# Head 0's scan: its four projection blocks spread over the head's whole window

## The chip, the cores and the metric

The kernel runs on one core of one Trainium2 chip. The metric is the device time of one execution in microseconds (us), median of several runs. A core has five engines with a queue each: TensorE (PE, matmuls and transposes into PSUM), VectorE (DVE), ScalarE (ACT), GpSimd (POOL) and SyncE (SP, which here only issues transfers). Each works through its own queue in order, and they wait for one another by semaphores. A matmul has its own row for loading the weights (PEld).

## The reference

Two layers of a trunk run over 640 tokens of width 1024: 128 context tokens and 512 latent tokens (five chunks of 128; chunk 0 is the context). Layer 0 mixes positions with a gated MLP. Layer 1 is a bidirectional gated DeltaNet with 8 heads, d_k = 128, d_v = 256:

```python
qkv = jax.nn.silu(short_conv(qkv, conv_w)).astype(jnp.float32)   # width 5, centred
q = l2norm(q.reshape(B, N, H_B, D_K)) * (D_K ** -0.5)
k = l2norm(k.reshape(B, N, H_B, D_K))
...
sol = lax.linalg.triangular_solve(lhs, rhs, left_side=True, lower=True)
...
def step(S, xs):
    qk_i, qd_i, kd_i, u_i, w_i, gl_i = xs
    v_new = u_i - jnp.einsum('bhcd,bhde->bhce', w_i, S)
    o = jnp.einsum('bhcd,bhde->bhce', qd_i, S) + jnp.einsum('bhij,bhje->bhie', qk_i, v_new)
    S = S * gl_i[..., None, None] + jnp.einsum('bhcd,bhce->bhde', kd_i, v_new)
    return S, o
```

Both directions are scanned and added; the sum is normalised, gated with SiLU(z), projected out, and added to the residual before the last layer norm.

## The kernel before

Layer 1 works head by head. Per head there are four projection blocks of 128 output columns (q = 0 for k, 1 for q, 2 and 3 for the two halves of v) and two more for the gate z (q = 4, 5). The parts are generators, each cut into pieces at its `yield`s:

- `project_head` and `project_z` (17 turns): a block is 2 halves of the tokens x 8 slices of the input width. One piece is `mm3`, three matmuls of 128x320 (L235, L236, L237) with weights split into a high and a low part. After each half ACT copies the sum out of PSUM (L831, L832, L834) into `xp`. In the second half the next block's weights are split, high part by ACT (L230) and low part by DVE or POOL (L231); the raw weights come through SP (L166) into three buffers.
- `conv`: ACT's first tap (L845), four taps on DVE (L848), a tanh on ACT (L851) and the SiLU's end on DVE (L853), which writes `cacc`.
- `post_k`, `post_q`, `post_v`: transposes of `cacc` on PE (L240, in `flip`), norms (sums of squares L876 on ACT, L246 on DVE, the power L248 on POOL, L905 on DVE), and a store of k and v per token (L907, L941).
- `chunk`, for three groups of chunks of a head: Gram matrices (L964), decays (L967, L969 on DVE) and the inverse of the triangular matrix in six doubling steps. One step is a product on PE (L1018), masks on DVE (L1023, tile Y), products on PE (L1029, L1030), a copy by ACT (L1033, tile TU). Corrections and the matrices G (L1003, L1042, L1048 to L1076) stand before and after the steps.
- `scan`, in five steps of two units (one per direction): PE reads the state (L1113), DVE makes r (L1116), PE applies G (L1126, L1127), DVE updates the state and the output (L1135, L1141, L1121). SP loads the state (L1093) and v (L1098); `chunk` loads the decays ex (L958) and kn (L961).

`stages()` lays these parts on a time axis whose unit is one head's window: window w holds the scan of head w, the chunks of head w + 1, the projections of head w + 2, and the end of head w - 1. The projection blocks of a window lie in equal slots, from `START[w + 2]` sixths of the window to its end; `conv` begins when its block ends, one sixth long, and the `post` part one sixth later. `turns()` sorts all pieces by their time, and the generators are called in that order. For PE and SP this order of calls is the queue's order (`manual_schedule`); the queues of DVE, ACT and POOL are put in order by the framework from the same program. The weights are loaded in the order in which blocks stand on the axis.

The window of head 0 (w = 0) has four blocks, those of head 2, since ZW places z blocks at w = -1 and from w = 1 on; windows 1 to 5 have six.

Of the kernel before, what the change touches and what calls it, by code (L numbers as in the profile page):

```python
# [77 lines left out]


ZW, ZPOS = (-1, 1, 2, 3, 4, 5, 6, 6), 0  # L80
START = 2, 0.3, 1
PIECES = {"scan": 24, "chunk": 40, "norm_o": 4, "gate_z": 4, "conv": 8, "post_k": 13,
          "post_q": 7, "post_v": 5, "gates": 7, "gates_e": 26, "residual": 17}

# [1 line left out]
def stages():  # L86
# [5 lines left out]
    for w in range(-2, H + 1):  # L92
# [7 lines left out]
        else:  # L100
            slots[ZPOS:ZPOS] = zs
        start = START[w + 2] if w + 2 < len(START) else 0
        wide = (n - start) / len(slots) if slots else 0
# [1318 lines left out]
```

## Time and profile before

| | us |
|---|---|
| median of 3 runs | 1349.68 |
| the runs | 1349.72, 1349.68, 1346.47 |
| the profiled execution | 1356.16 |
| its span (first to last instruction) | 1354.3 |
| PE busy | 1285.2 (95%) |
| DVE, ACT, POOL busy | 852.5, 601.4, 509.1 |

The profile's page gives the busy time of each engine; its other views give who waited for whom, the busy time and the granted PE clock of any stretch, and the instructions in order of time. Times in these views are us from the start of the span. PE's queue reaches head 0's window shortly before 670 us, and the next window's scan begins at 752 us (the first L1126 there starts at 752.29). Matmuls are pipelined: the distance between the starts of two of them says more than the length given for one.

### The profile page before, as it was taken

The numbers are of one execution on the slowest core, as the hardware profiler recorded it, in microseconds if no ns is written. First come the engines' busy times: TensorE is split into PE (matmuls) and PEld (weight loads), VectorE is DVE, ScalarE is ACT, GpSimd is POOL, SyncE is SP. The second block draws the span as 40 slices with busy tenths as digits, with TensorE's granted clock in tenths as the row PEclk, the third lists the DMA queues.
The fourth block names the chain that finished last, engine by engine and source line by source line (L and its number), as shares of the span: only waits on it lengthen the run. The fifth ranks groups of instructions, "written<-read, shape, count | busy, mean of one in ns | idle before, by whom it ended". The sixth has DMA issues, their size and how long they took to land. (4 is left out here: it accounts for less than half of the span.)

```text
span 1354.3 us, 22840 instructions
## 1 busy us (share of the span) xinstructions
PE 1285.2 (95%) x8773; PEld 1139.6 (84%) x8773; DVE 852.5 (63%) x1599; ACT 601.4 (44%) x1432; POOL 509.1 (38%) x503
## 2 busy tenths in 40 slices
PE   7999999999999998998989999999999999989996
PEld 4688899999997887787878999989899998877785
DVE  3664644444446566798667677686777767656357
ACT  2333522222224334675636555564555556453230
POOL 0221322222223433355243636356474745520014
PEclk9999999999999999999989999999999999999998
DMA  8512233333335323143122322324243243545732
GB/s 337 168 63 86 93 134 125 125 125 125 125 125 203 124 82 141 63 125 95 50 84 73 122 87 64 106 86 153 82 133 113 82 129 90 157 124 166 260 117 78
DMA packets 90254, 163.18 MB, mean 120 GB/s; under 512 B 9088, under 2 KB 55456, under 8 KB 90016
## 3 DMA queue, kind: packets, MB, share of 16 engines
q1 hardware_dynamic: 88704, 156.99, 35.3%
q10 hardware_dynamic: 1440, 4.72, 1.0%
q8 instruction: 69, 1.13, 0.3%
q14 instruction: 41, 0.34, 0.1%
HBM read 135.97 MB, written 25.71 MB: 119 GB/s over the span
## 5 line engine op out<-in xcount | busy, mean ns | idle before, releaser
L231 POOL TENSOR_TENSOR wlo<-wraw,whi 128x256 fp32r<-128x256 f32 (+1 forms) x188 | 198.4, 1078 | 249.7 <-ACT whi L230 249.6
L235 PE MATMUL pp<-hThi,whi 128*128 128x320 f32 (+1 forms) x784 | 278.8, 356 | 0.2 <-ACT hThi L230 0.2
L237 PE MATMUL pp<-hTlo,whi 128*128 128x320 f32 (+1 forms) x784 | 243.4, 311 | 0.4 <-POOL hTlo L231 0.4
L236 PE MATMUL pp<-hThi,wlo 128*128 128x320 f32 (+1 forms) x784 | 242.9, 310 | 0.0
L230 ACT CAST whi<-wraw 128x256 fp32r<-128x256 f32 (+1 forms) x262 | 142.9, 594 | 86.3 <-PE pacc L236 60.2
L235 PE MATMUL pacc<-hThi,whi 128*128 128x320 f32 x512 | 159.6, 312 | 0.0
L237 PE MATMUL pacc<-hTlo,whi 128*128 128x320 f32 x512 | 158.3, 309 | 0.0
L236 PE MATMUL pacc<-hThi,wlo 128*128 128x320 f32 x512 | 158.2, 309 | 0.0
L848 DVE SCALAR_TENSOR_TENSOR cacc<-xp,convw,cacc 128x642 f32<-128x642 f32 x128 | 137.1, 1071 | 31.2 <-ACT cacc L845 29.7
L235 PEld LDWEIGHTS pp<-hThi,whi 128*128 128x128 f32 (+1 forms) x784 | 148.0, 189 | 3.7 <-ACT hThi L230 0.3
L236 PEld LDWEIGHTS pp<-hThi,wlo 128*128 128x128 f32 (+1 forms) x784 | 147.7, 188 | 3.9
L237 PEld LDWEIGHTS pp<-hTlo,whi 128*128 128x128 f32 (+1 forms) x784 | 146.6, 187 | 1.6 <-POOL hTlo L231 0.7
L231 DVE TENSOR_TENSOR wlo<-wraw,whi 128x1024 fp32r<-128x1024 f32 (+1 forms) x74 | 89.6, 1222 | 65.2 <-ACT whi L230 65.0
L248 POOL TENSOR_TENSOR rs<-ve,mhalf 128x1 f32<-128x1 f32 (+2 forms) x39 | 40.1, 1028 | 176.1 <-DVE ve L246 172.8
L235 PEld LDWEIGHTS pacc<-hThi,whi 128*128 128x128 f32 x512 | 96.1, 188 | 3.1 <-issue 2.2
L236 PEld LDWEIGHTS pacc<-hThi,wlo 128*128 128x128 f32 x512 | 96.1, 188 | 0.0
L237 PEld LDWEIGHTS pacc<-hTlo,whi 128*128 128x128 f32 x512 | 96.1, 188 | 0.0
L256 POOL TENSOR_SCALAR gsq<-gsq 128x320 f32<-128x320 f32 (+1 forms) x52 | 27.7, 533 | 136.5 <-ACT gsq L255 135.6
L257 DVE TENSOR_TENSOR gsq<-pacc,gsq 128x320 f32<-128x320 f32 (+1 forms) x52 | 29.1, 565 | 73.7 <-POOL gsq L256 73.6
L255 ACT ACTIVATE gsq<-pacc 128x320 f32<-128x320 f32 (+1 forms) x52 | 25.7, 499 | 107.8 <-PE pacc L237 103.8
L1033 ACT CAST TU<-pt 128x512 f16<-128x512 f32 (+1 forms) x120 | 57.2, 526 | 30.0 <-PE pt L1030 27.6
L235 PE MATMUL pacc<-whi,hThi 128*128 128x512 f32 x160 | 64.1, 412 | 5.5 <-ACT whi L230 4.3
(334 smaller groups left out, 2987.8 us busy)
## 6 DMA issues: line engine op xcount, KB each, us to landing
wraw<-in_w_b SPq DMA_DIRECT2D x48, 512.0 KB
wraw<-in_w_ada SPq DMA_DIRECT2D x37, 512.0 KB
wraw<-in_w_uz SPq DMA_DIRECT2D x32, 512.0 KB
v<-kvd SPq DMA_DIRECT2D x72, 128.0 KB
wraw<-in_a_wo SPq DMA_DIRECT2D x16, 512.0 KB
wraw<-in_b_wo SPq DMA_DIRECT2D x16, 512.0 KB
kvd<-nat SPq DMA_DIRECT2D x24, 320.0 KB
cacc<-yd SPq DMA_DIRECT2D x24, 320.0 KB
```

Of the source, the lines that this page charges most:

```text
L230: self.nc.scalar.copy(hi, src)
L231: (e_lo or self.nc.vector).tensor_tensor(lo, src, f32(hi), op=ALU.subtract)
L235: mm(out, l_hi, r_hi, start=start, stop=False)
L236: mm(out, l_lo, r_hi, start=False, stop=False)
L237: mm(out, l_hi, r_lo, start=False, stop=stop)
L248: nc.gpsimd.tensor_tensor(r, ve, self.mhalf[:, 0:n], op=ALU.pow)
L255: nc.scalar.activation(sq, u, AF.Square)
L256: nc.gpsimd.tensor_scalar(sq, sq, GB, 1.0, op0=ALU.mult, op1=ALU.add)
L257: nc.vector.tensor_tensor(sq, u, sq, op=ALU.mult)
L848: nc.vector.scalar_tensor_tensor(acc, xp[:, i : i + PADN], w[:, i : i + 1], acc, op0=ALU.mult, op1=ALU.add)
L1033: nc.scalar.copy(part, p.rearrange("p s k t (j b) -> p s (k t j) b", b=b))
```

## The change

One number: the third entry of `START` goes from 1 to 0.

```diff
 ZW, ZPOS = (-1, 1, 2, 3, 4, 5, 6, 6), 0
-START = 2, 0.3, 1
+START = 2, 0.3, 0
 PIECES = {"scan": 24, "chunk": 40, "norm_o": 4, "gate_z": 4, "conv": 8, "post_k": 13,
```

For window 0 the four blocks had slots of 1.25 sixths (1.0 to 2.25, to 3.5, to 4.75, to 6.0) and now have 1.5 sixths (0 to 1.5, to 3.0, to 4.5, to 6.0). The convolutions of the first three follow at 1.5, 3.0 and 4.5 in place of 2.25, 3.5 and 4.75; the last block ends as before. No instruction is added or removed by intent; outside window 0 the axis is the same.

PE, from the second pair of Gram matrices (L964) of head 1's chunks in the window, over the scan's first units. Before:

```order
L964 MATMUL pt_6507<-kq_5849 128x2x128 x2
L1126 MATMUL ps_6510<-v_6470,G_1036_6329 128x256
L1127 MATMUL ps_6510<-v_6470,G_1036_6329 128x256
L1126 MATMUL ps_6513<-v_6470,G_1036_6329 128x256
L1127 MATMUL ps_6513<-v_6470,G_1036_6329 128x256
L1003 LDWEIGHTS A_1072_6500
L1003 MATMUL pt_6545<-id_759_4865,A_1072_6500 128x128
```

Now (pp is the PSUM sum of a projection block, pp_6455 and pp_6556 are the two halves of head 2's k block):

```order
L964 MATMUL pt_6531<-kq_5849 128x2x128 x2
L1126 MATMUL ps_6534<-v_6476,G_1036_6329 128x256
L1127 MATMUL ps_6534<-v_6476,G_1036_6329 128x256
L1126 MATMUL ps_6537<-v_6476,G_1036_6329 128x256
L1127 MATMUL ps_6537<-v_6476,G_1036_6329 128x256
L235 MATMUL pp_6455<-hThi_64,whi_6399 128x320
L236 MATMUL pp_6455<-hThi_64,wlo_6400 128x320
L237 MATMUL pp_6455<-hTlo_65,whi_6399 128x320
L235 MATMUL pp_6556<-hThi_64,whi_6399 128x320
L236 MATMUL pp_6556<-hThi_64,wlo_6400 128x320
L237 MATMUL pp_6556<-hTlo_65,whi_6399 128x320
```

Seven pieces of the first half now stand ahead of this L964 (between it and the L1064 before it), where there was none; five more follow up to the transposes of head 1's last v block (L240 on cacc), where there was one. From that L240 to the end of the window 52 pieces are left in place of 63.

DVE, at the convolution (L848, L853) of that same block and the decays of head 1's chunks (L967, L969, L974). Before:

```order
L967 TENSOR_TENSOR ge_1078_6517<-pt_6507,ex_6455 128x256
L848 SCALAR_TENSOR_TENSOR cacc_6453<-xp_766_4887,convw_4867,cacc_6453 128x642
L969 TENSOR_TENSOR pe_1079_6519<-pt_6507,ex_6455 128x256
L848 SCALAR_TENSOR_TENSOR cacc_6453<-xp_766_4887,convw_4867,cacc_6453 128x642
L974 SCALAR_TENSOR_TENSOR A_1080_6521<-ge_1078_6517,beta_4873,masks_4857 128x128
```

Now:

```order
L848 SCALAR_TENSOR_TENSOR cacc_6459<-xp_766_4887,convw_4867,cacc_6459 128x642 x3
L967 TENSOR_TENSOR ge_1080_6546<-pt_6531,ex_6461 128x256
L848 SCALAR_TENSOR_TENSOR cacc_6459<-xp_766_4887,convw_4867,cacc_6459 128x642
L969 TENSOR_TENSOR pe_1081_6548<-pt_6531,ex_6461 128x256
L974 SCALAR_TENSOR_TENSOR A_1082_6550<-ge_1080_6546,beta_4873,masks_4857 128x128 x4
L853 SCALAR_TENSOR_TENSOR cacc_6459<-xp_766_4887,cacc_6459 128x642
L1141 TENSOR_TENSOR o_6478<-o_6478,ps_6537 128x256
```

Three of the four taps stand ahead of the decays, and the scan's L1141, which stood ahead of L853, stands behind it. Later in the window one L246 (of head 2's k) stands between the second and the third of three L1023, where it stood behind all three, and one L848 stands right ahead of an L1023 of a late inversion step.

SP, where the scan's and the chunks' first loads are issued. Before:

```order
L961 DMA kn_1058_6457<-kvd_4835 128x128
L1093 DMA S_6466<-in_state 128x256
L1093 DMA S_6468<-in_state 128x256
L1098 DMA v_6470<-kvd_4834 128x256
L166 DMA wraw_6314<-in_w_b 128x1024
L941 DMA kvd_4835<-nat_6343 640x1x128
```

Now:

```order
L166 DMA wraw_6314<-in_w_b 128x1024
L166 DMA wraw_6453<-in_w_b 128x1024
L958 DMA ex_6461<-ed_4833 128x5x128
L961 DMA kn_1060_6463<-kvd_4835 128x128
L1093 DMA S_6472<-in_state 128x256
L1093 DMA S_6474<-in_state 128x256
L1098 DMA v_6476<-kvd_4834 128x256
L941 DMA kvd_4835<-nat_6343 640x1x128
```

Two weight blocks now go ahead of these loads, where one went behind them; the second (wraw_6453) takes the buffer of a block whose low part POOL splits, and waits for that. The load of ex, which stood further ahead, stands among them.

## The prediction

> **What bounds the kernel now.** I read the page first, for the engine that is nearly always busy, then the waits of that engine, then its time around the largest one.
>
> ```profile
> span 1354.3 us, 22840 instructions
> PE 1285.2 (95%) x8773; PEld 1139.6 (84%) x8773; DVE 852.5 (63%) x1599; ACT 601.4 (44%) x1432; POOL 509.1 (38%) x503
> ```
>
> TensorE (PE) is busy for 95% of the span, the next engine for 63%. The kernel gets shorter where PE waits or runs slowly. The change moves work in head 0's scan, so I asked for busy time from 669 us (its first matmuls) on, and for PE's waits there. Columns of the first view: window, its length, busy us (count) of PE, PEld, DVE, ACT and POOL, granted PE clock, DMA share, GB/s; of the second: who waited for whom, total us, times, longest.
>
> ```profile
> 669.00:740.00 71.00, 61.20 (x481) 55.29 (x480) 51.27 (x106) 38.03 (x105) 27.80 (x27) 0.93 0.26 81
> 690.00:740.00 50.00, 47.24 (x420) 43.75 (x418) 35.71 (x79) 26.57 (x73) 17.34 (x17) 1.00 0.29 88
> 740.00:820.00 80.00, 78.64 (x626) 73.47 (x626) 56.11 (x121) 45.40 (x132) 37.24 (x41) 1.00 0.28 90
> ```
>
> ```profile
> PE px L240 <- DVE cacc L853: 6.7, 1, 6.7
> PE pt L1029 <- DVE Y L1023: 1.8, 1, 1.8
> PE pt L1048 <- DVE U L1042: 0.9, 1, 0.9
> PE pt L1074 <- DVE T L1067: 0.4, 1, 0.4
> ```
>
> From 669 to 740 us PE stands idle for 71.0 - 61.2 = 9.8 us, and one wait makes 6.7 of them: the transposes (L240) of head 1's last block wait for the end of its convolution (L853) on VectorE (DVE). The next 80 us, where projection matmuls lie between the scan's pieces from the first on, lose 1.4 us. The 669 stretch also has a granted clock of 0.93:
>
> ```profile
> 677.00:678.00 1.00, 0.00 (x0) 0.00 (x0) 1.00 (x2) 0.02 (x1) 1.00 (x2) 0.97 0.88 209
> 678.00:682.00 4.00, 0.00 (x0) 0.00 (x0) 4.00 (x5) 0.74 (x1) 3.69 (x5) 0.50 0.52 177
> 682.00:688.00 6.00, 5.66 (x18) 4.76 (x19) 2.96 (x6) 2.23 (x6) 2.86 (x2) 0.50 0.00 0
> 688.00:689.00 1.00, 1.00 (x6) 0.83 (x6) 0.39 (x2) 0.47 (x1) 0.00 (x0) 0.91 0.00 0
> ```
>
> The clock halves 0.97 us into the 677 window and is full again 0.18 us into the 688 window. PE works from 682.34 to 688.18 at half clock: 5.84 us for 2.9 us of work. So the one stall costs 6.7 + 2.9 = 9.6 us, 0.7% of the span.
>
> **The change part by part.** *Fill moved into the stall.* One projection piece (L235 to L237, three matmuls) takes from one L235 to the next; the timeline of PE (start, us, line):
>
> ```profile
> 667.28 0.30 PE L235 MATMUL pp<-hThi,whi 128*128 128x320 f32 x1
> 667.72 0.31 PE L235 MATMUL pp<-hThi,whi 128*128 128x320 f32 x1
> ...
> 669.49 0.65 PE L964 MATMUL pt<-kq 128*128 128x256 f32 x2
> ...
> 675.00 0.39 PE L235 MATMUL pp<-hThi,whi 128*128 128x320 f32 x1
> ...
> 682.34 1.11 PE L240 MATMUL px<-ident,cacc 128*128 128x128 f32 x4 [6.66 <-DVE cacc L853]
> ```
>
> That is 0.44 us. In the order of before, one piece stands between L1064 and the waiting L240; in the changed order 12 do. So 11 x 0.44 = 4.8 us of PE work move ahead of the wait. Their weights are no new wait: in the old order their first piece already ran at 675.00, and the split that makes them ended on DVE at 660.7:
>
> ```profile
> 659.26 1.43 DVE L231 TENSOR_TENSOR wlo<-wraw,whi 128x256 fp32r<-128x256 f32 x4
> ```
>
> *When PE now gets to L240.* From 669.49 to 675.00 PE had 5.5 us, 0.4 of it the wait for T, so 5.1 us of work. With 12 pieces it is 5.1 + 5.3 = 10.4 us: L240's turn comes at 679.9, where it came at about 675.7.
>
> *When its input is ready.* DVE and ScalarE (ACT) before the wait:
>
> ```profile
> 672.52 0.84 ACT L845 ACTIVATE cacc<-xp,convw 128x642 f32<-128x642 f32 x1
> 673.39 0.42 DVE L967 TENSOR_TENSOR ge<-pt,ex 128x256 f32<-128x256 f32 x1 [1.76 <-PE pt L964]
> ...
> 680.18 0.41 DVE L1141 TENSOR_TENSOR o<-o,ps 128x256 f32<-128x256 f32 x1
> 680.51 1.78 DVE L853 SCALAR_TENSOR_TENSOR cacc<-xp,cacc 128x642 f32<-128x642 f32 x1
> ```
>
> DVE works without a gap from 673.39 to 682.29: 8.9 us. In the new order L967 waits for a later matmul (its L964 comes after 7 pieces instead of none, 7 x 0.44 = 3.1 us less the 0.4 of waiting that they fill), but three L848 stand ahead of it, which need only L845, and L1141 goes behind L853. The same 8.9 us less L1141's 0.4 start with L848 at 673.4 and end at 681.9. The wait that is left is 681.9 - 679.9 = 2.0 us, 4.7 us less than now. Bounds: L853 took 1.78 us here and 0.83 us at 736.91 (below), so 1.0 us if it runs unhindered; 2.9 us if the later L967 lets DVE idle for as long as one L848 (0.88, at 718.47 below). I take 2.0: **-4.7 us**. The 0.4 us wait for T goes too, since pieces now stand before L1074: **-0.4 us**.
>
> ```profile
> 680.34 1.26 POOL L989 TENSOR_TENSOR A<-A,ident 128x512 f16<-128x512 f32 x1 [0.23 <-DVE A L974]
> 736.91 0.83 DVE L853 SCALAR_TENSOR_TENSOR cacc<-xp,cacc 128x642 f32<-128x642 f32 x1 [0.27 <-ACT xp L851]
> ```
>
> The long L853 starts while GpSimd (POOL) runs L989; the short one runs with POOL idle. [...] The sum keeps 1.78.
>
> *The clock.* With 2.0 us of waiting in place of 6.7 I take the half-clock stretch as gone: **-2.9 us**. It is the least sure term, and a rival below.
>
> *What the fill leaves behind.* The 4.8 us of pieces are missing between the steps after L240: 52 in place of 63 up to the end of the window, about one in six. There PE waited for 50 - 47.24 = 2.8 us. A step of the chunk inversion goes L1018, L1023 on DVE, L1029, L1033 on ACT, next L1018; where PE's filled time is longer than DVE's or ACT's, a missing piece costs nothing; where it is not, all 0.44 us come back as waiting. The one step that already waits shows how:
>
> ```profile
> 718.08 0.47 DVE L1121 SCALAR_TENSOR_TENSOR o<-ps,scal,o 128x256 f32<-128x256 f32 x1
> 718.47 0.88 DVE L848 SCALAR_TENSOR_TENSOR cacc<-xp,convw,cacc 128x642 f32<-128x642 f32 x1
> 719.26 0.94 DVE L1023 TENSOR_TENSOR Y<-pt,wm 128x256 f16<-128x256 f32 x3
> ```
>
> Convolution and scan updates stand ahead of the three L1023 in DVE's queue. The new order has two places like it that the old one has not: L246, which waits for four sums of squares on ACT, stands before the last of three L1023, and an L848 stands ahead of the L1023 of a late step. I price each at 1 us, and a third at the same for what I do not see: **+3.0 us**. Bounds: 0 (all slack) and 4.8 (every removed piece comes back).
>
> *SyncE's queue.* The load of a weight block (L166) now stands ahead of ex, kn, S, S and v for the scan, and waits for POOL's split that frees its buffer:
>
> ```profile
> 651.36 4.14 POOL L231 TENSOR_TENSOR wlo<-wraw,whi 128x256 fp32r<-128x256 f32 x4 [12.70 <-ACT whi L230]
> 660.78 0.69 ACT L986 ACTIVATE M<-kn,scal 128x128 f32<-128x128 f32 x2
> 663.25 0.37 ACT L1039 CAST U<-pt 128x256 f16<-128x256 f32 x1 [1.28 <-PE pt L1064]
> 725.75 0.42 SPq L166 DMA_DIRECT2D wraw<-in_w_b  x1
> 731.00:732.00 1.00, 1.00 (x15) 0.88 (x14) 1.00 (x4) 0.35 (x1) 1.00 (x2) 1.00 0.15 51
> ```
>
> The split ends at 655.5, and only then do the six loads go out. The same row of loads, in the same order, left SyncE (SPq) from 725.75 on, and its last bytes moved in the 731 window, where 51 GB/s are left: under 6 us. So all have landed by 661.5. The first to need one is ACT's L986 (kn), whose turn comes at 660.78; behind it ACT idles 1.28 us before L1039, which PE needs. A kn that lands by 661.5 is hidden by that: **0**. Were it later than 662.1, every us would reach PE.
>
> *Sum.* -4.7 - 0.4 - 2.9 + 3.0 = -5.0 us: a span of 1349.3. The profiled execution took 1356.16 us, 1.9 more than its span, and lies 6.5 above the median of 1349.68; a difference of this kind has no reason to scale with that, so I take it off the median: **1344.7 us**.
>
> **The rivals.** *All slack.* None of the removed pieces is missed: the +3.0 becomes 0, 1341.7 us. For it: in the old order one step in the whole window waits for L1023. Against: the two places in DVE's new order.
>
> *All given back.* Each removed piece comes back as waiting, +4.8 in place of +3.0: 1346.5 us. For it: the scan's own chain (L1113, L1116, L1126, L1135) is the same length as before; against: PE has 47.24 busy us of 50 there, so steps are paced by PE and not by the chain.
>
> *The clock falls all the same.* A wait before another transpose shows it (the row of 718 us holds the 1.8 us wait for L1023):
>
> ```profile
> 541.50 1.97 PE L240 MATMUL ptr<-ident,r 128*128 128x128 f32 x8 [2.68 <-DVE oh L621]
> 541.00:545.00 4.00, 3.50 (x16) 2.89 (x16) 2.74 (x10) 3.59 (x8) 2.88 (x3) 0.57 0.32 114
> 718.00:720.00 2.00, 0.27 (x7) 0.27 (x7) 2.00 (x6) 0.49 (x2) 0.65 (x1) 1.00 0.00 0
> ```
>
> After 2.7 us of waiting the mean clock over 4.0 us was 0.57: half of it for 3.4 us. After 1.8 us it stayed at 1.00. My 2.0 us lies between. If it falls so, up to half of 3.4 is lost: 1344.7 + 1.7 = 1346.4 us. [...]
>
> *DVE becomes the bound* (the slower side). The window then holds three convolutions in full, each closer to the inversion steps. If in each of the eight steps after L240 the L1023 stand behind such work as the one at 719.26, PE waits 1.8 us eight times: 14.4 in place of 3.0, 1344.7 + 11.4 = 1356.1 us. It decides from 8.0 / 8 = 1.0 us a step, where the gain of 8.0 us (4.7 + 0.4 + 2.9) is used up. Against: DVE is busy 35.71 of 50 us; with the window some 8 us shorter that would be 85%.
>
> **How the numbers follow.** Forecast (with waits after L240 of 1.5 to 4 us, so 1343.2 to 1345.7) 0.45; all slack 0.13; all given back 0.17; clock falls 0.17; DVE bound 0.08. What can be told from no change is 0.3%, 4.05 us: faster means below 1345.6. To it belong three quarters of the forecast (its upper end and the spread of the runs before, 1346.47 to 1349.72, take the rest), all of the all-slack case and a sixth of the next two: 0.34 + 0.13 + 0.05 = 0.52. Slower than 1353.7 is most of the last case, 0.07. The rest, 0.41, is the same. The range goes from 1340.5 (1.2 under the all-slack case, if L240's wait falls to its lower bound) to 1350.0 (given back and clock together, 1348.2, with the spread of the runs).
>
> **What would show it.** Right: PE's wait for L853 before L240 between 1.0 and 2.9 us; the granted clock 1.00 from 669 to 740; new waits of PE on L1023 of about 1 us, 5 to 6 us of idle time in that window's later part, and the same waits as now after it; the six loads issued in one row behind a POOL split, with no wait of ACT's L986. Wrong: a wait for L853 of 4 us or more, or the clock at 0.50 behind it; PE waits of over 8 us in all after L240; PE waiting for L1048 early on behind a late kn; a total that moves although this window does not.

## The result, and the profile after

| | before | changed kernel |
|---|---|---|
| median of 6 runs each, us | 1349.70 | 1342.11 |
| the runs, us | 1346.47 to 1352.97 | 1340.34 to 1344.92 |
| ratio, with its 95% interval | | 0.9937 [0.9923, 0.9952] |
| profiled execution and its span, us | 1356.16, 1354.3 | 1341.76, 1340.0 |

The change makes the kernel 6.5 to 10.4 us faster (the interval times 1349.7 us); the forecast was 5 us (1344.7, within 1340.5 to 1350.0). The direction was right, the size too small. One further execution of the changed kernel, in the run e9_after below, took 2101.59 us at a mean granted clock of 0.56; the ratios are those of the other executions.

The two profiled executions differ by more than the medians, 14.4 us, because the one of before lay 6.5 us above its median. To tell the change from that, I take one stretch of the program in every profile: from the start of the 158th L235 of a projection (tile pp, weights whi on the right side) to the start of the 317th. It holds head 0's whole window and begins before the first reordered piece; outside it PE has the same order in both kernels. PE alone, in the columns window, its length, busy us (count), granted clock, DMA share, GB/s; before and after:

```profile
655.86:804.26 148.40, 137.80 (x1098) 0.97 0.25 78
```

```profile
650.54:790.64 140.10, 136.17 (x1099) 1.00 0.29 89
```

The stretch is **8.3 us** shorter. That is the change; it agrees with the ratio (0.63% of 1349.7 us is 8.5 us). The other 6 us between the two profiles lie outside it. PE's waits in it, after (the four rows of before that the prediction shows, and 0.6 us for L1030, are their counterpart):

```profile
PE pt L1018 <- DVE TU L1005: 1.1, 1, 1.1
PE px L240 <- DVE cacc L853: 0.8, 1, 0.8
PE pt L1030 <- DVE Y L1023: 0.6, 1, 0.6
PE pt L1029 <- DVE Y L1023: 0.6, 2, 0.3
PE pt L1048 <- ACT U L1039: 0.5, 1, 0.5
```

The 6.7 us before L240 have become 0.8, and nothing of that size has come in their place: idle time in the stretch falls from 10.6 to 3.9 us. The 71 us that answer to the prediction's first window (all five engines) have a full clock:

```profile
664.00:735.00 71.00, 67.75 (x541) 61.58 (x541) 54.22 (x119) 44.85 (x130) 33.23 (x33) 1.00 0.25 73
```

PE was busy for 61.20 us there and is now for 67.75. Around the stall, in order of time on PE, DVE and POOL (start, us, engine, line; in brackets the idle time ahead of it):

```profile
669.45 1.02 PE L964 MATMUL pt<-kq 128*128 128x256 f32 x4
...
675.34 0.66 PE L240 MATMUL px<-ident,cacc 128*128 128x128 f32 x4 [0.76 <-DVE cacc L853]
```

```profile
667.88 3.38 DVE L848 SCALAR_TENSOR_TENSOR cacc<-xp,convw,cacc 128x642 f32<-128x642 f32 x3 [1.25 <-ACT cacc L845]
671.18 0.41 DVE L967 TENSOR_TENSOR ge<-pt,ex 128x256 f32<-128x256 f32 x1
...
674.47 0.81 DVE L853 SCALAR_TENSOR_TENSOR cacc<-xp,cacc 128x642 f32<-128x642 f32 x1
675.20 0.41 DVE L1141 TENSOR_TENSOR o<-o,ps 128x256 f32<-128x256 f32 x1
```

```profile
674.62 1.80 POOL L989 TENSOR_TENSOR A<-A,ident 128x512 f16<-128x512 f32 x1 [0.75 <-DVE A L974]
```

Times of the two profiles are 5.32 us apart at the stretch's start (655.86 and 650.54). On the clock of before, PE's turn at L240 comes at 675.34 - 0.76 + 5.32 = 679.9, where the forecast put it to the tenth. L853 ends at 675.28 + 5.32 = 680.6, 1.3 us earlier than forecast: it starts 0.15 us ahead of POOL's L989 and takes 0.81 us (1.78 before), and this time L989 is the long one, with 1.80 us (1.26 before).

### The profile page after: what moved, and what is told of

It reads as the page before. It is cut to its first block, busy times and chain, and to the rows that moved or that the text cites. A ratio compares the mean times of both kernels' runs of the same rounds, so it can differ in the third digit from the quotient of the medians.

```text
span 1340.0 us, 22836 instructions
## 1 busy us (share of the span) xinstructions
PE 1277.5 (95%) x8773; PEld 1133.2 (85%) x8773; DVE 851.0 (64%) x1599; ACT 600.6 (45%) x1432; POOL 509.9 (38%) x503
## 5 line engine op out<-in xcount | busy, mean ns | idle before, releaser
L235 PE MATMUL pp<-hThi,whi 128*128 128x320 f32 (+1 forms) x784 | 279.2, 356 | 0.2 <-ACT hThi L230 0.2
L235 PE MATMUL pacc<-hThi,whi 128*128 128x320 f32 x512 | 159.6, 312 | 0.0
L848 DVE SCALAR_TENSOR_TENSOR cacc<-xp,convw,cacc 128x642 f32<-128x642 f32 x128 | 137.1, 1071 | 32.0 <-ACT cacc L845 30.6
L235 PEld LDWEIGHTS pp<-hThi,whi 128*128 128x128 f32 (+1 forms) x784 | 147.5, 188 | 3.8 <-ACT hThi L230 0.3
L235 PEld LDWEIGHTS pacc<-hThi,whi 128*128 128x128 f32 x512 | 96.1, 188 | 3.1 <-issue 2.2
L235 PE MATMUL pacc<-whi,hThi 128*128 128x512 f32 x160 | 63.1, 406 | 5.5 <-ACT whi L230 4.1
```

The lines of the kernel that those rows point to most:

```text
L235: mm(out, l_hi, r_hi, start=start, stop=False)
L848: nc.vector.scalar_tensor_tensor(acc, xp[:, i : i + PADN], w[:, i : i + 1], acc, op0=ALU.mult, op1=ALU.add)
```

## The experiments

All runs are compared with the kernel before on the same chip. "Stretch" is the one defined above: 148.4 us before, 140.1 after. The diffs are cut (`...`), and each is against the kernel that its row names, before or changed; those of `START` are against the kernel before.

| run | what it is | ratio to before | stretch, us | wait at L240, us |
|---|---|---|---|---|
| e5_warm | before, PE kept busy in the stall | 0.9988 [0.9975, 1.0000] | 146.8 | 0 |
| e1_post_late | before, L240 later | 0.9992 [0.9977, 1.0007] | 146.3 | 0 |
| e2_half | START[2] = 0.5 | 0.9970 [0.9955, 0.9986] | 145.8 | 3.8 |
| e6_dve_order | changed, L853 late on DVE | 0.9951 [0.9934, 0.9968] | 144.7 | 3.7 |
| e4_fill_only | changed, conv and post as before | 0.9921 [0.9903, 0.9938] | 140.0 | 0.8 |
| e3_front | changed, last sixth empty | 0.9967 [0.9950, 0.9983] | 144.6 | 0 |
| e7_thin | changed, pieces earlier still | 0.9940 [0.9924, 0.9955] | 138.2 | 0 |
| e8_thinner | the same, more so | 0.9961 [0.9947, 0.9975] | 143.6 | 0 |
| s1 | START = 2, 0, 0 | 0.9949 [0.9931, 0.9967] | 140.0 | 0.8 |
| s2 | START = 1.5, 0, 0 | 0.9969 [0.9955, 0.9983] | 140.0 | 0.8 |
| e9_after | the changed kernel again | 0.9932 [0.9918, 0.9946] | 140.0 | 0.8 |
| e10_thin | e7_thin again | 0.9928 [0.9914, 0.9942] | 138.4 | 0 |

### The clock by itself

```diff
-    def flip(self, src, c0):
+    def flip(self, src, c0, warm=0):
...
+        for c in [c - warm for c in warms] + list(range(n)):
+            self.transpose(p[:, c % n, :], self.ident if c < 0 else src(c0 + c), self.ident)
...
+            p = self.flip(lambda c: s[:, tok(c)], c0, 60 * ((h, q, c0) == (1, 3, 1)))
```

> The kernel before, with 60 more transposes of the identity into the same PSUM tile just ahead of the waiting L240 (their results are overwritten), about 6.2 us of PE work that stands where PE waits now. The end of L853 on VectorE stays where it is. Theory (the clock falls because PE is idle, and costs 2.8 us by itself): the granted clock stays at 1.00 from 669 to 740 us, L240 starts at the same distance from the scan's start, and the time falls by 2.5 to 3 us. Rival (the half clock costs nothing that lasts, since PE would wait for VectorE behind it anyhow): clock 1.00, new waits of 2 to 3 us behind L240, the time the same within 0.7 us.

PE of this kernel in order of time, and its granted clock:

```profile
673.07 6.71 PE L240 MATMUL px<-ident 128*128 128x128 f32 x60
679.93 0.66 PE L240 MATMUL px<-ident,cacc 128*128 128x128 f32 x4
```

```profile
653.42:697.44 44.02, 43.48 (x347) 1.00 0.26 82
...
715.00:719.00 4.00, 3.97 (x22) 0.57 0.25 67
```

The real transposes start 679.93 - 653.42 = 26.51 us into the stretch (26.48 in the kernel before), so VectorE was no earlier. The clock stayed full, and PE reached the 197th piece after 44.02 us; the kernel before needs

```profile
655.86:702.67 46.81, 39.77 (x287) 0.89 0.25 77
```

46.81 us. The half clock behind the stall costs **2.8 us** by itself, as the theory has it: nothing behind L240 waits longer for it. The ratio shows less (1.6 us, interval 0 to 3.4), and in this profile the reason can be seen: at 715 us a wait of 1.8 us for L1023, as long as it is in the kernel before, was followed by 3.4 us at half clock, which it was not there. Of the 2.8 us, 1.2 were lost again by that in this execution.

### The place of L240

```diff
-                add(("post_k", "post_q", "post_v", "post_v")[q], (h, q), (i + POST_AT) / n,
-                    (i + POST_AT + (KLEN if q == 0 else POST_LEN)) / n)
+                add(("post_k", "post_q", "post_v", "post_v")[q], (h, q), (i + POST_AT + 0.8 * ((h, q) == (1, 3))) / n,
+                    (i + POST_AT + 0.8 * ((h, q) == (1, 3)) + (KLEN if q == 0 else POST_LEN)) / n)
```

> The kernel before, with only the post part of head 1's last block (its transposes L240) 0.8 sixths later on the axis, so that 12 projection pieces stand ahead of it as in the changed kernel; no piece is moved. Theory (PE lacks work that does not depend on VectorE there; VectorE's row from L967 to L1005 is what is late): the wait before L240 goes, but PE now runs on to the next product that needs VectorE, L1018 on TU, and waits there 4 to 6 us; the clock halves as before; gain 0 to 2 us. Rival (the place of this one L240 is the whole cause): no wait over 2 us in its neighbourhood, clock full, gain 7 to 9 us.

PE's largest waits, and its time at half clock:

```profile
PE ps L1113 <- DVE o L1141: 3.7, 1, 3.7
PE pt L1029 <- DVE Y L1023: 1.8, 1, 1.8
PE pt L1018 <- DVE TU L1005: 1.5, 1, 1.5
```

```profile
679.52:686.35 6.83, 4.99 (x14) 0.50 0.29 104
```

The gain is 1.1 us by the ratio, whose interval holds no gain too, and 2.1 in the stretch. L240 waits no more, but 3.7 + 1.5 = 5.2 us of waiting come back at the next instructions that need VectorE. The first is one I had not named: L1113, which needs the PSUM tile that L1141 has still to read. Then comes L1018, as expected. So no single instruction is to blame: VectorE's row is late, and PE has nothing else to do. The rival falls.

### VectorE's order alone

```diff
-                add("conv", (h, q), (i + CONV_AT) / n, (i + CONV_AT + CONV_LEN) / n)
+                add("conv", (h, q), (i + CONV_AT) / n, (i + CONV_AT + CONV_LEN + 0.1 * ((h, q) == (1, 3))) / n)
```

> The changed kernel with one difference, on VectorE alone: the convolution of head 1's last block ends a tenth of a sixth later on the axis, so that L853 stands behind L1141 and L980, no longer right behind L974. PE, ScalarE, GpSimd and SyncE have the same order as in the changed kernel. Theory (what is left of the stall is VectorE's row alone, and L853's place in it carries a part of the gain): L853 ends 1.8 to 2.7 us later, PE's wait before L240 goes from 0.8 to 2.5 to 3.5 us, the clock may halve for one stretch of 3.4 us; time 1.8 to 4.5 us above the changed kernel. Rival (PE would wait at L1018 for TU anyhow, so L853's place is free): waits of L240 and L1018 together as in the changed kernel, time within 0.7 us of it.

DVE, then PE's wait, then the clock in PE's rows:

```profile
676.32 0.41 DVE L1141 TENSOR_TENSOR o<-o,ps 128x256 f32<-128x256 f32 x1
676.65 1.63 DVE L980 TENSOR_TENSOR M<-pe,masks 128x512 f32<-128x512 f32 x1
678.21 1.78 DVE L853 SCALAR_TENSOR_TENSOR cacc<-xp,cacc 128x642 f32<-128x642 f32 x1
```

```profile
PE px L240 <- DVE cacc L853: 3.7, 1, 3.7
```

```profile
677.52:680.93 3.41, 0.89 (x7) 1.00 0.82 267
680.93:684.34 3.41, 3.41 (x10) 0.50 0.00 0
```

With every projection piece where the changed kernel has it, two instructions ahead of L853 on VectorE take back 4.6 of the 8.3 us: 2.9 us of waiting, and most of the rest the half clock behind it. Both the wait of 3.7 us and the 4.6 us lie a little above the theory's bounds (3.5 and 4.5). L853 ends 3.0 us later in the stretch than in the changed kernel, and 1.0 of them is its own length: POOL's L991 starts at 677.81, 0.4 us ahead of it, and L853 takes 1.78 us in place of 0.81. The rival (L853's place is free) falls. The gain is therefore not that of the pieces alone. With L853 in this place, which is even behind L980 (in the kernel before it is ahead of L980), the pieces are worth 148.4 - 144.7 = 3.7 us.

### Pieces without the new convolution times

```diff
-                i += wide - 1
+                i = 1.25 * (q + 1) if w == 0 else i + wide - 1
```

> The changed kernel's projection pieces, with the convolutions and post parts of head 2 at their old times on the axis. Theory (the pieces ahead of the stall make the gain, and the new places in VectorE's order cost nothing): same time as the changed kernel within 1 us, 7.5 to 9 us under the kernel before, waits after L240 of 2 to 3 us in all. Rival (the earlier convolutions and post parts carry a part of the gain, by taking work off VectorE later in the window): 2 to 4 us slower than the changed kernel, with waits on L1023 of 1 us and more.

```profile
655.64:795.63 139.99, 135.25 (x1098) 1.00 0.28 89
```

The stretch is as short as that of the changed kernel (140.10). VectorE's order at the stall is the same as there, and the new places of head 2's convolutions and post parts neither gain nor cost in sum. Within the sum they do move something: here PE is idle for 4.7 us and busy for 135.25, in the changed kernel idle for 3.9 and busy for 136.17. Of the idle time 4.0 us come after L240, where the theory had 2 to 3.

### Half of the change

```diff
-START = 2, 0.3, 1
+START = 2, 0.3, 0.5
```

> The third entry of START at 0.5: 7 pieces ahead of L240 where the kernel before has 1 and the changed kernel 12. Theory (each piece ahead takes its own 0.44 us off the wait, and the row of VectorE is as long as before): L853 behind GpSimd's L989 at 1.8 us, wait before L240 3 to 4 us, the clock halves for at least 3.4 us; time between the two kernels, 2 to 5 us under the kernel before. Rival (the gain comes as a whole as soon as the three L848 stand ahead of L967): wait under 1.2 us, clock full, time within 1 us of the changed kernel.

```profile
PE px L240 <- DVE cacc L853: 3.8, 1, 3.8
```

```profile
677.88 1.77 DVE L853 SCALAR_TENSOR_TENSOR cacc<-xp,cacc 128x642 f32<-128x642 f32 x1
```

```profile
675.29:678.70 3.41, 0.59 (x5) 1.00 0.39 115
678.70:682.11 3.41, 2.41 (x9) 0.50 0.00 0
682.11:685.52 3.41, 3.41 (x11) 0.50 0.00 0
```

6 pieces more than before are 2.6 us of PE work, and the wait falls by 6.7 - 3.8 = 2.9 us. VectorE has the old order (L1141, then a long L853), and the clock still halves, for two stretches of 3.41 us in place of three. Gain 2.6 us in the stretch: the first half of the pieces brings a third of the gain, and the second half, with which VectorE's order turns, two thirds.

### How much can be taken away behind the stall

The three kernels place the four blocks of the window in other slots; the last two keep the changed kernel's times for convolutions and post parts.

e3_front:

```diff
-        wide = (n - start) / len(slots) if slots else 0
+        wide = (n - start - (w == 0)) / len(slots) if slots else 0
```

e7_thin, and e8_thinner with `(0, 1, 2, 3)[k], (1, 1, 1, 3)[k]` in the same place:

```diff
-        for i, (kind, h, q) in enumerate(slots):
-            i = start + i * wide
+        for k, (kind, h, q) in enumerate(slots):
+            i, wide = ((0, 1, 2, 4)[k], (1, 1, 2, 2)[k]) if w == 0 else (start + k * wide, wide)
...
-                i += wide - 1
+                i = 1.5 * (k + 1) - 1 if w == 0 else i + wide - 1
```

> The changed kernel with its four blocks in five sixths of the window (slots of 1.25 sixths from 0), so that the last sixth holds no projection piece. Theory (PE waits wherever the scan and the chunks stand without pieces between them): L240 of head 1's last block waits less than 1 us as in the changed kernel, and 4 to 8 us of waits appear in the last sixth; time 4 to 8 us above the changed kernel, so about that of the kernel before. Rival (pieces are missed only at the window's start, where the chunks' first decays and a convolution fall together): waits in the last sixth under 1.5 us, time within 1.5 us of the changed kernel.

> The changed kernel with the pieces of window 0 earlier still: slots of 1, 1, 2 and 2 sixths in place of four of 1.5; convolutions and post parts keep the times of the changed kernel. 18 pieces stand ahead of L240 of head 1's last block (12 in the changed kernel), and from the scan's first L1126 on r to the window's end 26 are left (35; 40 in the kernel before). Theory (the steps after the stall have slack, a lacking piece costs little): the 0.8 us wait before L240 goes, waits after it rise by under 1.5 us, time within 1 us of the changed kernel. Rival (the forecast's price, up to 0.44 us for each of the 9 lacking pieces): waits after it rise by 3 to 4 us, time 2 to 4 us above the changed kernel.

> As the last, with slots of 1, 1, 1 and 3 sixths: again 18 pieces ahead of L240, and 19 from the scan's first L1126 on r to the window's end (35 in the changed kernel). Theory (slack up to a point, which the run with no piece in the last sixth passed): waits rise by 2 to 4 us, time 1 to 4 us above the changed kernel. Rival (each of the 16 lacking pieces comes back): 6 to 7 us above it, no gain left against the kernel before.

The stretches of e7_thin and e8_thinner, and the waits of e3_front in its last sixth:

```profile
655.12:793.27 138.15, 135.36 (x1098) 1.00 0.29 90
```

```profile
655.63:799.23 143.60, 136.46 (x1098) 1.00 0.28 87
```

```profile
PE pt L1064 <- DVE R L1060: 1.7, 1, 1.7
...
PE pt L1048 <- DVE U L1042: 1.2, 1, 1.2
```

e3_front: 2.9 us in these two waits and 6.8 us at half clock from the second one on, 4.5 us above the changed kernel. Where no piece stands, PE waits, at the end of the window as at its start. The theory holds for the time; the two waits alone are less than its 4 to 8 us, and the half clock makes up the rest.

e7_thin: by the trace, 11 pieces fewer than in the changed kernel are left behind the scan's first L1126 on r, and 9 (4.0 us of PE work) behind the second group of them, from which the count given above goes. The stretch is not longer but 1.9 us shorter: the L240 wait is gone, and PE's idle time is 2.8 us in place of 3.9. So the forecast's price for a lacking piece is refuted up to this point.

e8_thinner: 16 pieces fewer (by the same count) cost 3.5 us, which lies in the first theory's range, but not for the reason given. The wait of 3.0 us is for L1023, and VectorE's rows ahead of it show what is late:

```profile
718.67 0.48 DVE L1116 SCALAR_TENSOR_TENSOR r<-ps,neg,v 128x256 f32<-128x256 f32 x1 [0.88 <-DMA v<-kvd]
...
719.47 0.94 DVE L1023 TENSOR_TENSOR Y<-pt,wm 128x256 f16<-128x256 f32 x3
```

```profile
712.76 0.52 SPq L907 DMA_DIRECT2D kvd<-nat  x1
713.34 2.21 SPq L1098 DMA_DIRECT2D v<-kvd  x4
```

L1116 waits for a load of v (L1098), which stands in SyncE's queue behind the store of head 2's k (L907). The store leaves 712.76 - 655.63 = 57.1 us into the stretch; in the changed kernel it leaves at 703.13 - 650.54 = 52.6. In e8_thinner 15 more pieces stand ahead of the transposes (L240 of head 2's k) on which the store rests. By this trace the next bound in this window is thus a store on SyncE. Whether the steps of the inversion would have waited for one another at 16 pieces fewer, had v come in time, stays open.

### The same change one window earlier

```diff
-START = 2, 0.3, 1
+START = 2, 0, 0
```

This is s1; s2 has `START = 1.5, 0, 0`.

> START = 2, 0, 0: the same change in the window before as well (the chunks of head 0, the projections of head 1), where the changed kernel waits 1.8 us before L240 for L853 and 2.1 and 0.9 us before L1029. Theory (the same mechanism on a smaller scale): the L240 wait of that window falls by 1.5 to 1.8 us and its lost clock, when there is one, goes; time 1 to 3 us under the changed kernel. Rival (that window has one empty slot of 0.3 sixths only, and its waits for L1023 come from VectorE's own row): time within 1 us of the changed kernel.

> START = 1.5, 0, 0: as the last, and head 0's own blocks spread from 1.5 sixths in the first window of layer 1. Theory (PE waits of 1.0 to 1.4 us in that window, for L905 and L796, stand where no pieces are): 0.5 to 2 us under the last. Rival (head 0's blocks then come before their weights or their input are ready, so PE waits at their first piece): 1 us above the last or more.

PE's waits of s1 in the later part of that window:

```profile
PE pt L1029 <- DVE Y L1023: 2.0, 1, 2.0
PE pt L1029 <- DVE xp L859: 2.0, 1, 2.0
PE px L240 <- DVE nat L905: 1.4, 1, 1.4
PE px L240 <- DVE cacc L853: 1.0, 1, 1.0
```

Wait before L240: 1.0 us where the changed kernel has 1.8. But the second L1029 waits 2.0 us instead of 0.9, and L240 on nat 1.4 instead of 0.9. Nothing is gained, as the rival had it for s1. s2 is the slowest of the three: L240 on nat waits up to 2.6 us in the first window, the theory's gain does not come.

### Side by side

> The changed kernel again, beside the next one on the same chip. Theory: 0.993 to 0.994 of the kernel before; the stretch from the 158th to the 317th projection piece 140.0 us within 0.3, no half clock in it. Rival (the first profile was a lucky one, and waits of 0.8 and 1.1 us can cost the clock there): a stretch of 141.5 us or more with a half clock in it.

> The kernel with slots of 1, 1, 2 and 2 sixths again, beside the changed kernel on the same chip. Theory (its stretch is 1.9 us shorter than that of the changed kernel, and everything else the same): stretch 138.2 us within 0.3, time 1 to 2.5 us under the changed kernel. Rival (what the stretch gains is lost again outside it): stretch as before, time within 0.7 us of the changed kernel or above.

The changed kernel repeats its stretch to 0.1 us and e7_thin to 0.2 us, both with a full clock. e7_thin's is 1.9 us the shorter in the first profiles and 1.6 in these; the ratios (0.9928 and 0.9932) cannot tell the two apart. It beats the kernel before in the timing, and the changed kernel in the trace alone.

## Why the prediction was right, and where it was off

The sum was -4.7 - 0.4 - 2.9 + 3.0 = -5.0 us. In the stretch it is -8.3:

| term | forecast | measured | from |
|---|---|---|---|
| wait before L240 | -4.7 | -5.9 | 6.66 to 0.76 us |
| wait for T | -0.4 | -0.4 | gone |
| half clock | -2.9 | -2.8 | e5_warm |
| waits after L240 | +3.0 | -0.4 | 3.5 to 3.1 us of idle time |
| what the sum had not | 0 | +1.2 | the rest |

*When PE gets to L240*: right to 0.1 us. *When its input is ready*: the idle and queued work was right to 0.3 us, the length of L853 wrong by 1.0. I kept 1.78 us and had named 0.83 us as the other end; the row of after says 0.81. So the wait that is left, 0.8 us, lies below the 1.0 to 2.9 that I gave. Which of the two it is goes, in the profiles, with who starts first. In the kernel before, POOL's L989 starts 0.17 us ahead of L853 here, takes 1.26 us, and L853 takes 1.78 (1.77 in e1_post_late and e2_half). In the changed kernel L853 starts first and takes 0.81 us (so in e4_fill_only), and L989 takes 1.80. The two profiles hold 14 more pairs of an L853 and an L989 that overlap: in each, L853 starts 0.15 or 0.16 us ahead and takes 0.81 or 0.82, and L989 takes 1.80 to 2.42. No run changes this order and nothing else, so it was not shown that the order makes the length.

*The clock*: right in size, and right that the wait left over would not set it off. That was luck in part, since the 2.0 us that I had forecast could have: in e5_warm a wait of 1.8 us was followed by 3.4 us at half clock, in e6_dve_order and e2_half waits of 3.7 and 3.8 us by 3.4 and 6.8 us of it, and the last section has a slot with 1.66 us of idle time that was followed by it and one with 1.91 us that was not. (The half clock set in at 677.94 us, 0.94 us into its window and not 0.97 as the prediction reads.)

*What the fill leaves behind*: this is the step that failed. I priced three places at 1 us each, +3.0 us, and the idle time fell by 0.4. At the first, L246 between the L1023, VectorE waited 0.3 us for ScalarE, and PE lost 0.2 us. At the second, the L848 ahead of an L1023, PE waited 0.3 us. The third stood for what I did not see, and there is such a wait: 1.1 us of L1018 for L1005, which the kernel before does not have. What the sum left out is that waits go as well: L1048 waits 0.5 us in place of 0.9, and the wait of 1.8 us before L1029, at the place that I scaled from, went. It went in e4_fill_only too, where the convolutions have their old times, so their move is not the cause, and what is I did not separate. e7_thin shows that still fewer pieces cost nothing. The row that I scaled from, an L1023 behind an L848, told what one collision costs; I had no row that said how much of that the new places would repeat.

*SyncE's queue*: right. The six loads left between 650.21 and 653.54 us, behind POOL's split that ended at 650.18; no wait for kn, S or v came of it at the window's start. The term that the same queue does hold is at the other end of the window (e8_thinner).

*What the sum had not*: 1.2 us more busy time on PE. A projection matmul right behind other work takes 0.26 us to the next start, one behind its like 0.146 us; the stretch has 74 such changes in place of 69, which makes 5 x 0.12 = 0.6 us. The rest is in the rows of L1030: counted up to the next start on PE, L1030 makes 4.2 us in the stretch, where it makes 3.5 in the kernel before and in e4_fill_only. After:

```profile
702.01 0.22 PE L1030 MATMUL pt<-TU,Y 128*128 128x128 f16 x1
702.28 0.22 PE L1029 MATMUL pt<-Y,TU 128*128 128x64 f16 x2
```

The next L1029 starts 0.27 us behind this L1030, where 0.06 us is usual; the one at the first of the places above, L246, starts 0.23 us behind its L1030. I take these for short waits that count as busy time. They stand at the new places on VectorE, and e4_fill_only, which does not have these places, does not have them either; it is idle for longer instead.

Of the rivals, *all slack* (1341.7 us) came nearest to the 1342.1 measured, on a chance of 0.13. That it lies so near is luck in part: in its sum, too, L240's wait is 1.2 us too long, and the 1.2 us of busy time that no sum had make up for that. *All given back* and *DVE becomes the bound* were wrong. *The clock falls all the same* did not occur here, and did where the wait was 3.7 us.

## What to carry to other kernels

A wait on the busiest engine is priced by the row of the engine that it waits for: where work is moved into the wait, ask first how long that row will be in the new order, and which of its instructions will then start ahead of another engine's (here L853 took 0.81 us where it started ahead of POOL's L989, and 1.78 us where it started behind it). A price for "fewer fillers later" needs a row that shows the later steps waiting, and the waits that the same move takes away belong in the same sum; here the two came to nearly nothing, until a store elsewhere became late (e8_thinner) or a part of the window had no filler at all (e3_front). And a long wait on TensorE can cost more than its length: here 6.7 us of waiting took 2.8 us more by the clock.

## What the runs showed that was not expected

**The half clock came in slots of 3.41 us.** In the profiled execution of the kernel before, the stretches at half clock begin at 421.94, 541.41, 677.94, 1131.91 and 1346.95 us; the distances from the first are 35, 75, 208 and 271 times 3.413 us. The stretch from 421.94 is 3.41 us long, the one from 677.94 10.24. In the profile of the changed kernel they begin at 962.43 and 1334.49 us, 109 times 3.413 us apart. So in each of these two executions they lie on one grid, and whether a wait of 2.7 us cost the clock went with how it lay on it. The clearest case is a wait that neither kernel's change touches, 2.68 us before L240 on ptr. Before:

```profile
538.00:541.41 3.41, 0.82 (x8) 1.00 1.02 341
541.41:544.82 3.41, 3.32 (x14) 0.50 0.27 106
```

After:

```profile
532.35:535.76 3.41, 1.50 (x14) 1.00 0.86 293
535.76:539.18 3.42, 2.65 (x19) 1.00 0.46 168
539.18:542.59 3.41, 2.58 (x20) 1.00 0.39 156
```

Before, the wait falls into one slot, PE is busy for 0.82 us of it, and the next slot runs at half clock. After, it is split over two, and the clock stays. In e9_after, which is the changed kernel again, it falls into one slot, and the clock halves:

```profile
534.43:537.85 3.42, 0.75 (x8) 1.00 1.00 323
537.85:541.26 3.41, 3.41 (x16) 0.50 0.23 93
```

So the slot ahead of a half clock was not idle throughout: PE was busy for 0.82 us of it in the kernel before, for 0.75 in e9_after, and in the changed kernel for 1.22 us of another:

```profile
959.02:962.43 3.41, 1.22 (x11) 1.00 0.05 16
962.43:965.84 3.41, 3.41 (x12) 0.50 0.01 2
```

Where the edge lies could not be settled with these counts. In the kernel before, a slot with 1.66 us of idle time (418.53 to 421.94 us) is followed by half clock and one with 1.82 us (609.68 to 613.09) is not; nor is the one with 1.91 us in the changed kernel (532.35 to 535.76, above). And one of the slots at half clock in the kernel before (1131.91) follows one with 0.80 us of idle time only, which stays open.

**The scatter between executions is in part this.** Of the 25 runs of the kernel before that the first experiments share, span and lost clock (one less the mean granted clock, times the span) go together with a correlation of 0.66 and a slope of 1.06 us per us; the correlation leaves more than half of the scatter to other causes, or to the clock's three digits (0.001 of it is 1.35 us of the span). A difference of one profile to another of a few us is, before it is explained by an edit, to be looked for in the clock's record.
